# Queue orders pinned from a walk over the traced program, and the sums of a step by seven in two half tiles

## The chip, the cores and the metric

The kernel runs on one core of one Trainium2 chip. The metric is the device time of one execution in microseconds (us), lower is better. The engines are called TensorE (PE in the profile, its weight loader PEld), VectorE (DVE), ScalarE (ACT), GpSimd (POOL) and SyncE (SP, which issues the DMAs of the weights).

## The reference

The reference is a trunk of two decoder layers over one sequence of 256 tokens with 2048 channels, all in float32. Cut to what matters:

```python
def reference(x, ...):
    h = x
    for i in range(2):
        hn = rmsnorm(h, norm_mix[i])
        if i == 0:      # causal means over 2/4/8/16 tokens in 4 channel groups, minus hn, times pool_w
            mix = pool_mixer(hn, pool_w[0], pool_scale[0])
        else:           # 8 heads of differential attention with distance penalties
            mix = diff_attention(hn, w_qkv[0], ..., subln_g[0], w_o[0], lambda_init)
        h = h + mix
        h = h + swiglu(rmsnorm(h, norm_ffn[i]), w_gate[i], w_up[i], w_down[i])
    return rmsnorm(h, final_norm)

def swiglu(h, wg, wu, wd):      # 2048 -> 2 x 5632 -> 2048
    return (jax.nn.silu(h @ wg) * (h @ wu)) @ wd
```

Nearly all of the work is in matrix products with large weights: gate, up and down of two layers (5632 wide), the queries, keys and values (2048 to 6144) and the output projection (2048 to 2048).

## The kernel before, in words

**Numbers in halves.** A float32 operand is split into a high half, rounded to the type fp32r (`whi`, made by ScalarE's copy), and a low half, the difference (`wlo`, made by VectorE). A product a·b becomes three products on TensorE: high·high, high·low and low·high, added up in one PSUM bank (`products`, L172 to L190; the matmul is L189, and each takes 128 rows by 512 columns).

**Steps.** `group` (L147) multiplies two blocks of 128 tokens by two blocks of 512 output columns. It goes through the contracted dimension in steps of 256, that is two blocks of 128. A weight step is one tile `raw` of 128 x 4 x 512 float32 (1 MiB) that holds its four blocks B12, B11, B22, B21; `load` (L116) fetches it by a DMA on SP's queue, into a pool with three buffers. A plain step takes the eight block products in the ordinary way, 8 x 3 = 24 matmuls, into four banks C11, C12, C21, C22. A step by seven (`seven`) forms seven products of sums of blocks (the scheme of Strassen and Winograd), 7 x 3 = 21 matmuls, into seven banks M1, M2, M6, M7, P5, P3, P4. The sums of the weight blocks T1 to T4 are made in float32 by `sums` (L128 to L134, VectorE, one instruction over two blocks, L130, and two over one, L132 and L133) in a tile `tsum` of 128 x 4 x 512, and split by `sum_halves` (L136) into `thi` (L139, ScalarE) and `tlo` (L140, VectorE), one instruction of 2048 columns each. `halves` (L121) splits the raw blocks (L124 ScalarE, L125 VectorE): 2048 columns in a plain step, 1536 in a step by seven, which does not need B12 alone. `combined` (L204) puts the seven or eight banks together on VectorE and ScalarE; of the banks M2, P3, P4 and X the plain steps are C11, C12, C21, C22.

**Buffers.** `raw`, `whi` and `wlo` have three buffers. `tsum` has one. `thi` and `tlo` have one in the feed-forward layers and two in the groups of attention (`bufs=2` in L599, L618 and L637). PSUM has eight banks; M1, M6, M7 and P5 are also the banks that `aux` (L83) hands out in turn for transposes and small products.

**Which steps are by seven.** In the feed-forward layers the steps 2, 4 and 6 of the eight (2 and 4 of six); in the first group of queries and keys, in the first of values and in the output projection 4 and 6; in the other three groups of queries and keys and the second of values the order of the steps is 0, 1, 3, 5, 4, 2, 6, 7 (`LATE`, L46), and 4, 2 and 6 are by seven, one after the other. There are 114 steps by seven in all.

**Stages.** The pooling mixer comes first (L288 to L436, up to some 60 us). A feed-forward layer (`ffn`, L466) goes in three chunks of 4, 4 and 3 groups of 512 hidden columns: for each group the products with gate and up (L483), silu and the product of both (L486, L487), and transposes of the result into operands `h` (`pair`, L254, transposes L259; a pair by seven also gets its own sums, L273 to L275, a high half L276 and a low half L277); after the groups of a chunk come the two halves of the down projection (L502). Attention (L527 to L643) has four groups of queries and keys with two heads each (`head`, L566, transposes L607, scores L576, transposes of the probabilities L561), two groups of values (L618, with L622 to L624 for the heads), and the output projection (L637). `finish` (L440) ends the last down projection for each of the two token blocks t: it adds the products to the residual in `x_tok` (L449), sums squares on ScalarE (L452), multiplies by the final gain into `ys` (L453; an earlier part of it in L516), works out the factor (L229 to L234), scales (L458, L461, L463) and issues the output DMAs (L459, L462, L464).

**What sets the order.** All engines run their queues in order. The kernel traces its instructions in program order; when the context closes, the framework's scheduler orders each engine's queue by priority, which is the program order, shifted by `tc.high_priority` (L429 and L432), and by when its own timing model takes an instruction as ready. So products of a later bank or step can stand ahead of earlier ones on TensorE. It then sets the semaphores. Within one PSUM bank the products stay in program order.

```python
for x, y in ((ah, hi), (ah, lo), (al, hi)):
    left[b] -= 1
    nc.tensor.matmul(ps[b], x, y[:, block], start=first, stop=(left[b] == 0))
    first = False
```

Of the kernel before, what the change touches and what calls it, by code (L numbers as in the profile page):

```python
# [2 lines left out]

# [6 lines left out]
F32 = mybir.dt.float32  # L10
F32R = mybir.dt.float32r
# [5 lines left out]
P = 128  # L17
# [8 lines left out]
EPS = 1e-6  # L26
WARM = 8
LATER = 70

WINDOWS = (2, 4, 8, 16)  # L30

# [19 lines left out]

A22, A21, A11, A12, S1, S3, S2, S4 = range(8)
T1, T3, T2, T4 = range(4)


@with_exitstack
def trunk_kernel(ctx, tc, x_n, gains, scale_in, final_in, subln, lam_in, band, counts_in, dist,
# [39 lines left out]
    def x_at(t, first, count=512):  # L97

        j, off = divmod(first, 512)
        return x_tok[:, j, t, off:off + count]  # L100
# [25 lines left out]
        return hi, lo  # L126

    def sums(pool, raw):  # L128
        t = pool.tile([P, 4, 512], F32, name="tsum")
        nc.vector.tensor_tensor(t[:, T1:T3 + 1], raw[:, B11:B22 + 1],  # L130
                                raw[:, B12:B12 + 1].broadcast_to([P, 2, 512]), ALU.add)
        nc.vector.tensor_tensor(t[:, T2], t[:, T1], raw[:, B22], ALU.add)  # L132
        nc.vector.tensor_tensor(t[:, T4], t[:, T2], raw[:, B21], ALU.add)  # L133
        return t  # L134

    def sum_halves(pool, t, bufs):  # L136
        hi = pool.tile([P, 4, 512], F32R, name="thi", bufs=bufs)
        lo = pool.tile([P, 4, 512], F32R, name="tlo", bufs=bufs)
        nc.scalar.copy(hi, t)  # L139
        nc.vector.tensor_tensor(lo, t, f32(hi), ALU.subtract)  # L140
        return hi, lo
# [298 lines left out]
    def finish(cs, ys, final_sb, ss):  # L440

        for t in range(2):
            part = tmp.tile([P, 64], F32, name="part", bufs=2)
            nc.vector.tensor_reduce(part[:, 0:1], ss[:, t, 0:2], AX.X, ALU.add)
            for b in range(2):
                for h in range(2):
                    first = 1024 + b * 512 + h * S
                    mine = slice(h * S, (h + 1) * S)
                    nc.vector.tensor_tensor(x_at(t, first, S), cs[t][b][:, mine], x_at(t, first, S), ALU.add)  # L449
# [3 lines left out]
                nc.vector.tensor_tensor(ys[1][:, t, b], x_at(t, 1024 + b * 512), final_sb[1][:, b * 512:(b + 1) * 512], ALU.mult)  # L453
# [4 lines left out]
            nc.scalar.activation(ys[1][:, t, 0], ys[1][:, t, 0], AF.Copy, scale=rt)  # L458
            nc.scalar.dma_start(out=out[rows, 1024:1536], in_=ys[1][:, t, 0])  # L459
            for b in range(2):  # L460
                nc.vector.tensor_scalar(ys[0][:, t, b], ys[0][:, t, b], rt, None, ALU.mult)  # L461
            nc.sync.dma_start(out=out[rows, 0:1024], in_=ys[0][:, t].rearrange("p b n -> p (b n)"))  # L462
            nc.vector.tensor_scalar(ys[1][:, t, 1], ys[1][:, t, 1], rt, None, ALU.mult)  # L463
            nc.sync.dma_start(out=out[rows, 1536:2048], in_=ys[1][:, t, 1])  # L464

    def ffn(layer, xq, ss, next_op, next_gain):  # L466

# [2 lines left out]
        with tc.tile_pool(name=f"ffn{layer}", bufs=1, reuse_waits="tile") as hp:  # L470
            g0 = 0
            ys = []
            for c, n in enumerate(CHUNKS):
# [19 lines left out]
                for o in range(2):  # L493
# [13 lines left out]
                    for b, t in ((0, 0), (0, 1), (1, 0), (1, 1)):  # L507
                        j = 2 * o + b
                        nc.vector.tensor_tensor(x_at(t, j * 512), cs[t][b], x_at(t, j * 512), ALU.add)
                        if last:  # L510
                            square_sum(ss_next, t, j)
                        if last and next_op is None:
                            if b == 0 and t == 0:
                                ys.append([hp.tile([P, 2, 2, 512], F32, name="y", tag=("tsum", "thi")[i]) for i in range(2)])
                                ys = ys[0]
                            nc.vector.tensor_tensor(ys[o][:, t, b], x_at(t, j * 512),  # L516
                                                    final_sb[o][:, b * 512:(b + 1) * 512], ALU.mult)
                        if last and t and next_op is not None:
                            transposed(next_op, j, next_gain, SEVEN_QKV)
# [8 lines left out]
    with tc.tile_pool(name="attn", bufs=1, reuse_waits="tile") as ap_, ExitStack() as heads:  # L528
# [67 lines left out]
        for g in range(4):  # L596

            order, by_seven = LATE if g else EARLY
            cs = combined(group([(xp[p], p in by_seven, w_qk[g, p]) for p in order], hq, bufs=2), hq)  # L599
            cs = scaled(cs, (qs_col, r_col))  # L600
            for u in range(2):
                qk = at.tile([P, 2, 2, S], F32, name="qk")
                for b in range(2):
                    tp = aux((P, 2, S))
                    for c in range(2):
                        for t in range(2):
                            nc.tensor.transpose(tp[:, c, t * P:(t + 1) * P],  # L607
                                                cs[t][b][:, (2 * u + c) * P:(2 * u + c + 1) * P], ident)
                    nc.scalar.copy(qk[:, b], tp)
                head(2 * g + u, qk)  # L610
# [4 lines left out]
        oT = [None] * NP  # L615
        for g in range(2):
            order, by_seven = LATE if g else EARLY
            cs = scaled(combined(group([(xp[p], p in by_seven, w_v[g, p]) for p in order], op_, bufs=2), op_), (r_col, r_col))  # L618
            for h in range(4 * g, 4 * g + 4):
                v = [cs[t][h % 4 // 2][:, h % 2 * E:(h % 2 + 1) * E] for t in range(2)]  # L620
                op = aux((P, 2, E))
# [12 lines left out]
                pair(oT[h], lambda i, t: on[:, t, i * P:(i + 1) * P], [gs[:, i:i + 1] for i in range(2)], h in SEVEN_O)  # L634
        xq = operand(SEVEN)
        for g in range(2):
            cs = combined(group([(oT[p], p in SEVEN_O, w_o[g, p]) for p in range(NP)], op_, bufs=2), op_)  # L637
            for b in range(2):
                j = 2 * g + b
                for t in range(2):  # L640
# [2 lines left out]
                transposed(xq, j, 4, SEVEN)  # L643

    ffn(1, xq, ss_next, None, None)


def _steps(w, left, right):
# [85 lines left out]
```

## Time and profile before

| what | value |
|---|---|
| median of 3 runs | 1837.09 us (1836.84 to 1837.28) |
| the profiled execution | 1837.09 us |
| its span, first to last instruction | 1835.3 us |
| TensorE busy in the span | 1823.0 us (99%), 8192 matmuls |
| VectorE busy | 1630.5 us (89%), 1692 instructions |
| ScalarE busy | 1048.7 us (57%), 1026 instructions |
| DMA engines | 193 GB/s of HBM traffic over the span |

TensorE's granted clock was 0.998 of full speed over the span. A row of the waits reads: who waited, for whom, us in total, times, longest. A row of the timeline reads: start, us, engine, line, operation, output and input with shapes, how many were merged, and in brackets the idle time before it and what ended it. TensorE's matmuls overlap in the profile (a 512-column one is shown with 0.39 us), so their pace is read from start to start. A row of groups ends with the busy time and the mean in ns, and with the idle time before the group.

### The profile page before, as it was taken

The page shows a single profiled execution, that of the slowest core. Times are in us where ns is not written, and L with a number is a line of the kernel's source. Part 1 is how long each engine was busy: PE and PEld are TensorE (multiplying, and loading weights), DVE is VectorE, ACT ScalarE, POOL GpSimd, SP SyncE. Part 2 cuts the span into 40 slices and gives each one's busy share as a digit, 9 for nine tenths or more (in the row PEclk, how much of TensorE's full clock was granted, in tenths as well). Part 3 has the DMA queues.
Part 4 walks back from the last instruction along what each step waited for, and adds up shares of the span by engine and source line. Part 5 has one row for each costly group of instructions (what it writes and reads, how often), then busy time and mean ns, then how long its engine had stood idle before and what let it go on. Part 6 is the DMA issues. An engine that isn't in the chain of part 4 may idle for free.

```text
span 1835.3 us, 20926 instructions
## 1 busy us (share of the span) xinstructions
PE 1823.0 (99%) x8192; PEld 1492.3 (81%) x8192; DVE 1630.5 (89%) x1692; ACT 1048.7 (57%) x1026; POOL 0.7 (0%) x6
## 2 busy tenths in 40 slices
PE   9999999999999999999999999999999999999997
PEld 6888888888888888888888888888888888888886
DVE  7999999889899899989988789889899899988986
ACT  6655544555554556666667665555554555555563
POOL 0000000000000000000000000000000000000000
PEclk9999999999999999999999999999999999999999
DMA  7555555555555555544554555555555545556552
GB/s 271 200 184 193 208 196 209 204 187 205 205 194 197 205 184 184 206 173 174 182 183 163 181 184 184 206 185 205 204 190 202 207 183 193 212 215 210 202 189 110
DMA packets 50930, 356.35 MB, mean 194 GB/s; under 512 B 6160, under 2 KB 6288, under 8 KB 8464
## 3 DMA queue, kind: packets, MB, share of 16 engines
q1 hardware_dynamic: 49968, 353.40, 53.5%
q10 hardware_dynamic: 864, 1.63, 0.2%
q8 instruction: 64, 1.05, 0.2%
q14 instruction: 34, 0.28, 0.0%
HBM read 352.90 MB, written 2.10 MB: 193 GB/s over the span
## 4 chain that ended last, share of the span: by engine, by line
PE 97%; DVE 1%; ACT 1%; DMA 0%; issue 0%; SPq 0%; DVEq 0%; ACTq 0%
PE b L189 93%; PE b L259 2%; PE b L576 1%; PE b L607 0%; DMA x_tok<-x_n 0%; PE b L368 0%; PE b L624 0%; PE b L622 0%; PE b L623 0%; PE b L561 0%; DVE wlo L354 0%; DVE xt_hl L252 0%; ACT sq L240 0%; DVE wlo L125 0%; DVE z L392 0%
## 5 line engine op out<-in xcount | busy, mean ns | idle before, releaser
L189 PE MATMUL b<-whi,xp 128*128 128x512 f32 x2784 | 899.4, 392 | 0.0
L124 ACT CAST whi<-raw 128x1536 fp32r<-128x1536 f32 (+1 forms) x328 | 578.7, 1764 | 549.6 <-PE b L189 450.4
L125 DVE TENSOR_TENSOR wlo<-raw,whi 128x1536 fp32r<-128x1536 f32 (+1 forms) x328 | 689.6, 2103 | 159.2 <-ACT whi L124 158.9
L189 PEld LDWEIGHTS b<-whi,xp 128*128 128x128 f32 x2784 | 520.1, 188 | 108.2 <-ACT e L272 0.4
L189 PE MATMUL b<-wlo,xp 128*128 128x512 f32 x1392 | 544.2, 391 | 0.0
L189 PE MATMUL b<-whi,h 128*128 128x512 f32 x1108 | 354.2, 390 | 0.0
L189 PEld LDWEIGHTS b<-wlo,xp 128*128 128x128 f32 x1392 | 261.5, 188 | 53.0
L140 DVE TENSOR_TENSOR tlo<-tsum,thi 128x2048 fp32r<-128x2048 f32 x114 | 260.6, 2286 | 8.3 <-ACT thi L139 8.3
L189 PEld LDWEIGHTS b<-whi,h 128*128 128x128 f32 x1108 | 207.5, 188 | 43.2
L139 ACT CAST thi<-tsum 128x2048 fp32r<-128x2048 f32 x114 | 217.6, 1908 | 19.7 <-DVE tsum L133 17.2
L189 PE MATMUL b<-thi,xp 128*128 128x512 f32 x640 | 223.4, 389 | 0.0
L189 PE MATMUL b<-wlo,h 128*128 128x512 f32 x554 | 215.8, 389 | 0.0
L130 DVE TENSOR_TENSOR tsum<-raw 128x1024 f32<-128x1024 f32 x114 | 139.1, 1220 | 2.1 <-DMA raw<-w_v 0.6
L189 PEld LDWEIGHTS b<-thi,xp 128*128 128x128 f32 x640 | 120.1, 188 | 24.7
L189 PE MATMUL b<-tlo,xp 128*128 128x512 f32 x320 | 125.9, 393 | 0.0
L189 PEld LDWEIGHTS b<-wlo,h 128*128 128x128 f32 x554 | 104.0, 188 | 21.3
L189 PE MATMUL b<-thi,h 128*128 128x512 f32 x240 | 83.7, 390 | 0.0
L133 DVE TENSOR_TENSOR tsum<-tsum,raw 128x512 f32<-128x512 f32 x114 | 78.5, 689 | 2.2
L132 DVE TENSOR_TENSOR tsum<-tsum,raw 128x512 f32<-128x512 f32 x114 | 78.1, 685 | 0.6
L189 PEld LDWEIGHTS b<-tlo,xp 128*128 128x128 f32 x320 | 60.0, 188 | 16.5 <-DVE tlo L140 4.4
L189 PE MATMUL b<-whi,oT 128*128 128x512 f32 x216 | 69.7, 395 | 0.0
L189 PEld LDWEIGHTS b<-thi,h 128*128 128x128 f32 x240 | 45.0, 188 | 9.5 <-ACT thi L139 0.4
(147 smaller groups left out, 1211.7 us busy)
## 6 DMA issues: line engine op xcount, KB each, us to landing
raw<-w_gu SPq DMA_DIRECT2D x176, 1024.0 KB, 4.8
raw<-w_down SPq DMA_DIRECT2D x88, 1024.0 KB, 4.8
raw<-w_qk SPq DMA_DIRECT2D x32, 1024.0 KB, 4.8
raw<-w_v SPq DMA_DIRECT2D x16, 1024.0 KB, 4.8
raw<-w_o SPq DMA_DIRECT2D x16, 1024.0 KB, 4.8
x_tok<-x_n SPq DMA_DIRECT2D x4, 512.0 KB, 6.9
w<-pool_w SPq DMA_DIRECT2D x4, 512.0 KB, 7.5
raw<-pool_w SPq DMA_DIRECT2D x2, 1024.0 KB, 11.1
```

What stands on the lines that cost most here:

```text
L124: nc.scalar.copy(hi[:, lo_block:], raw[:, lo_block:])
L125: nc.vector.tensor_tensor(lo[:, lo_block:], raw[:, lo_block:], f32(hi[:, lo_block:]), ALU.subtract)
L130: nc.vector.tensor_tensor(t[:, T1:T3 + 1], raw[:, B11:B22 + 1], raw[:, B12:B12 + 1].broadcast_to([P, 2, 512]), ALU.add)
L132: nc.vector.tensor_tensor(t[:, T2], t[:, T1], raw[:, B22], ALU.add)
L133: nc.vector.tensor_tensor(t[:, T4], t[:, T2], raw[:, B21], ALU.add)
L139: nc.scalar.copy(hi, t)
L140: nc.vector.tensor_tensor(lo, t, f32(hi), ALU.subtract)
L189: nc.tensor.matmul(ps[b], x, y[:, block], start=first, stop=(left[b] == 0))
L259: nc.tensor.transpose(ps[:, i, 1 - t if seven else t], src(i, t), ident)
L576: nc.tensor.matmul(sc[:, :nk], qk[:, 0, c, qb * P:(qb + 1) * P], qk[:, 1, c, :nk], start=True, stop=True)
```

## The change

The change has three parts.

1. **Orders.** At the end of the trace `in_order_of_need` takes the program's instructions as steps with the steps that each must wait for (`steps_of`: overlapping tiles, whole PSUM banks, buffers that come round again), gives each a duration (`Step`: how long it holds its engine and when its result is there, by engine, operation and size), and runs them in a list schedule (`walk`): the engine that is free first takes, of its steps that are ready, the one of the lowest rank. In the first round the rank is the program order. `due` then works out, backwards from TensorE's order, when each step's result is needed, and the walk is repeated (`ROUNDS = 2`) with that as the rank of VectorE, ScalarE and GpSimd, while TensorE and SP keep the program order. The order with the shortest end is pinned for PE, DVE, ACT and SP by a dependency from each instruction to the one before it on its queue.
2. **Halves of the sums.** `tsum`, `thi` and `tlo` become two tiles of two blocks each (T1 and T3, T2 and T4), each with its own instruction for the high and the low half and its own release. The pools of attention keep one buffer of each where they had two. The order of the seven products changes: M1, M2, P3, then the four on sums; and the four on sums first where the next step is by seven too.
3. **The final tiles** `ys` become one tile for each token block.

```diff
+PE, DVE, ACT, SP, POOL = (...)
+SIGNAL = {PE: 54, DVE: 36, ACT: 36, SP: 36, POOL: 36}
+AGAIN = 70
+SETTLES = {DVE: 36, ACT: 120}
+LANDING = 2100
+PER_MIB = 2500
+
+class Step:
+    def __init__(self, k, ins=None):
...
+        n = max(size(a) for a in list(ins.outs) + list(ins.ins) if hasattr(a, "ap"))
+        if self.dma:
+            self.share = PER_MIB * bytes_ / 2 ** 20
+            self.holds, self.lasts = (60 if self.engine == ACT else 330), LANDING + self.share
+        elif self.engine == PE:
+            n = size(ins.outs[0])
+            one = 110 if ins.is_transpose else 14 + n / 2.4 if "float32r" in str(ins.ins[0].dtype) else 14 + n / 0.6
+            self.holds, self.lasts = one, one + 163
+        elif self.engine == DVE:
...
+                self.lasts = 152 + n / (1.92 if ins.opcode == "TensorCopy" else 0.96)
+            self.holds = max(self.lasts - 80, 60)
+        elif self.engine == ACT:
+            self.lasts = 165 + n * 0.852
...
+def walk(steps, rank):
...
+    for _ in steps:
+        now, e = min((free[e] if able[e] else max(free[e], coming[e][0][0]), i)
+                     for i, e in enumerate(engines) if able[e] or coming[e])
+        e = engines[e]
+        while coming[e] and coming[e][0][0] <= now:
+            k = heapq.heappop(coming[e])[1]
+            heapq.heappush(able[e], (rank[k], k))
+        s = steps[heapq.heappop(able[e])[1]]
...
+        if len(waits) > 1 and ready[s.k] > free[e]:
+            now += AGAIN
+        start[s.k], free[e] = now, now + s.holds
...
+def due(steps, start):
+    by_start = sorted(steps, key=lambda s: start[s.k])
+    at, clock = {}, 0.0
+    for s in by_start:
+        if s.engine == PE:
+            at[s.k], clock = clock, clock + s.holds
+    limit = [0.0] * len(steps)
+    for s in reversed(by_start):
+        limit[s.k] = min([limit[k] - s.lasts - SIGNAL[steps[k].engine] for k in s.after] + [at.get(s.k, clock)])
+    return limit
+
+def in_order_of_need(tc):
+    steps = steps_of(list(tc.nc.cur_bb.bb.instructions))
+    rank = [float(s.k) for s in steps]
+    start, end = walk(steps, rank)
+    for _ in range(ROUNDS):
+        limit = due(steps, start)
+        rank = [float(s.k) if s.engine in (PE, SP) else limit[s.k] for s in steps]
+        again, span = walk(steps, rank)
+        if span < end:
+            start, end = again, span
+    order = mybir.DependencyInfo(mybir.DependencyClass.NoSync, mybir.DependencyReason.DATA)
+    for e in (PE, DVE, ACT, SP):
+        line = sorted((s for s in steps if s.engine == e), key=lambda s: start[s.k])
+        for one, two in zip(line, line[1:]):
+            tc.add_manual_dep(two.ins, one.ins.name, order, reason="order of need")
+    return start, end, steps
...
     def sums(pool, raw):
-        t = pool.tile([P, 4, 512], F32, name="tsum")
-        nc.vector.tensor_tensor(t[:, T1:T3 + 1], raw[:, B11:B22 + 1],
-                                raw[:, B12:B12 + 1].broadcast_to([P, 2, 512]), ALU.add)
-        nc.vector.tensor_tensor(t[:, T2], t[:, T1], raw[:, B22], ALU.add)
-        nc.vector.tensor_tensor(t[:, T4], t[:, T2], raw[:, B21], ALU.add)
-        return t
-
-    def sum_halves(pool, t, bufs):
-        hi = pool.tile([P, 4, 512], F32R, name="thi", bufs=bufs)
-        lo = pool.tile([P, 4, 512], F32R, name="tlo", bufs=bufs)
+        s, t = (pool.tile([P, 2, 512], F32, name=f"tsum{i}") for i in range(2))
+        nc.vector.tensor_tensor(s, raw[:, B11:B22 + 1], raw[:, B12:B12 + 1].broadcast_to([P, 2, 512]), ALU.add)
+        nc.vector.tensor_tensor(t[:, 0], s[:, 0], raw[:, B22], ALU.add)
+        nc.vector.tensor_tensor(t[:, 1], t[:, 0], raw[:, B21], ALU.add)
+        return s, t
+
+    def sum_halves(pool, t, bufs, i):
+        hi = pool.tile([P, 2, 512], F32R, name=f"thi{i}", bufs=bufs)
+        lo = pool.tile([P, 2, 512], F32R, name=f"tlo{i}", bufs=bufs)
...
-        for a, seven, src in steps:
-            if seven:
-                plan.append([(M1, [(A11, 0, B11)]), (M2, [(A12, 0, B21)]), (M6, [(S2, 1, T2)]), (M7, [(S3, 1, T3)]),
-                             (P5, [(S1, 1, T1)]), (P3, [(S4, 0, B22)]), (P4, [(A22, 1, T4)])])
+        for n, (a, seven, src) in enumerate(steps):
+            if seven and n + 1 < len(steps) and steps[n + 1][1]:
+                plan.append([(P5, [(S1, 1, 0)]), (M7, [(S3, 1, 1)]), (M6, [(S2, 2, 0)]), (P4, [(A22, 2, 1)]),
+                             (M1, [(A11, 0, B11)]), (M2, [(A12, 0, B21)]), (P3, [(S4, 0, B22)])])
+            elif seven:
+                plan.append([(M1, [(A11, 0, B11)]), (M2, [(A12, 0, B21)]), (P3, [(S4, 0, B22)]), (P5, [(S1, 1, 0)]),
+                             (M7, [(S3, 1, 1)]), (M6, [(S2, 2, 0)]), (P4, [(A22, 2, 1)])])
...
-                w.append(sum_halves(pool, t, bufs))
+                w += [sum_halves(pool, t[i], bufs, i) for i in range(2)]
...
-                                ys.append([hp.tile([P, 2, 2, 512], F32, name="y", tag=("tsum", "thi")[i]) for i in range(2)])
-                                ys = ys[0]
+                                ys.extend([hp.tile([P, 2, 512], F32, name="y", tag=f"{n}{i}") for i in range(2)]
+                                          for n in ("tsum", "thi"))
...
-            cs = combined(group([(xp[p], p in by_seven, w_qk[g, p]) for p in order], hq, bufs=2), hq)
+            cs = combined(group([(xp[p], p in by_seven, w_qk[g, p]) for p in order], hq, bufs=1), hq)
...
+    in_order_of_need(tc)
```

More of the change, by code (lines that the diff above doesn't have):

```diff
@@ L1 @@
+import heapq
 import math
@@ L28 @@
 LATER = 70
+ROUNDS = 2
 WINDOWS = (2, 4, 8, 16)
@@ new lines, in steps_of @@
+def steps_of(instructions):
+    steps, seen, slots, users, gates = [], {}, {}, {}, {}
+    open_, closed, pool_of = [], None, {}
+    for ins in instructions:
+        if ins.opcode == "TilePoolBoundary":
+            if ins.op == "release":
+                past = Step(len(steps))
+                past.before = {k for n in seen if pool_of.get(n) == open_[-1] for k in users[n]}
+                past.before |= {closed} if closed is not None else set()
+                closed = past.k
+                steps.append(past)
+                open_.pop()
+                continue
+            open_.append(len(pool_of))
+            pool_of.update((t.name, open_[-1]) for t in ins.bass_pool_tiles or ())
+            continue
+        if not any(hasattr(a, "bass_ap") for a in ins.outs):
+            continue
+        step = Step(len(steps), ins)
+        for writes, args in ((False, ins.ins), (True, ins.outs)):
+            for a in args:
+                ap = getattr(a, "bass_ap", None)
+                if ap is None or not hasattr(ap.tensor, "tag"):
+                    continue
+                t, dims = ap.tensor, [tuple(d) for d in ap.ap]
+                first = ap.offset % dims[0][0]
+                last = first + sum((c - 1) * s for s, c in dims[1:])
+                alone = writes
+                if t.space == PSUM:
+                    first, last, alone = 0, 511, True
+                if t.name not in seen:
+                    seen[t.name], users[t.name], gate = [], [], set()
+                    line = slots.setdefault(t.tag, [])
+                    bufs = t.bufs or t.tag_meta.bufs
+                    if len(line) >= bufs:
+                        gate.update(users[line[-bufs]])
+                    elif t.name in pool_of and closed is not None:
+                        gate.add(closed)
+                    if line:
+                        gate.add(users[line[-1]][0])
+                    line.append(t.name)
+                    gates[t.name] = gate
+                own = {k for f, l, w, k, _ in seen[t.name] if (w or alone) and f <= last and first <= l}
+                step.before |= own or gates[t.name]
+                step.reads.update(k for f, l, _, k, w in seen[t.name] if w and not writes and f <= last and first <= l)
+                if alone:
+                    seen[t.name] = [s for s in seen[t.name] if s[0] < first or s[1] > last or s[3] == step.k]
+                seen[t.name].append((first, last, alone, step.k, writes))
+                users[t.name].append(step.k)
+        step.before.discard(step.k)
+        steps.append(step)
+    for s in steps:
+        for k in s.before:
+            steps[k].after.append(s.k)
+    return steps
@@ new lines, in walk @@
+def walk(steps, rank):
+    missing = [len(s.before) for s in steps]
+    ready, start = [0.0] * len(steps), [0.0] * len(steps)
+    engines = (PE, DVE, ACT, SP, POOL)
+    free, wire = {e: 0.0 for e in engines}, 0.0
+    known, count = {e: {} for e in engines}, {e: 0 for e in engines}
+    place = [0] * len(steps)
+    able, coming = {e: [] for e in engines}, {e: [] for e in engines}
+    for s in steps:
+        if not s.before:
+            heapq.heappush(coming[s.engine], (0.0, s.k))
+    for _ in steps:
[6 more added lines that the diff above has]
+        s = steps[heapq.heappop(able[e])[1]]
+        waits = {}
+        for k in s.before:
+            t = steps[k].engine
+            if place[k] > max(waits.get(t, 0), known[e].get(t, 0)) and (t != e or e != PE):
+                waits[t] = place[k]
+        known[e].update(waits)
+        count[e] += 1
+        place[s.k] = count[e]
+        if len(waits) > 1 and ready[s.k] > free[e]:
+            now += AGAIN
+        start[s.k], free[e] = now, now + s.holds
+        end = now + s.lasts
+        if s.dma:
+            begin = max(now + s.holds, wire)
+            wire = begin + s.share
+            end = begin + s.lasts
+        for k in s.after:
+            t = steps[k].engine
+            if t != e or s.dma:
+                at = end + SIGNAL[t]
+            elif e == DVE or e == ACT and s.k in steps[k].reads:
+                at = end + SETTLES[e]
+            else:
+                at = now + s.holds
+            ready[k] = max(ready[k], at)
+            missing[k] -= 1
+            if not missing[k]:
+                heapq.heappush(coming[steps[k].engine], (ready[k], k))
+    return start, max(free.values())
@@ L617, in trunk_kernel @@
             order, by_seven = LATE if g else EARLY
-            cs = scaled(combined(group([(xp[p], p in by_seven, w_v[g, p]) for p in order], op_, bufs=2), op_), (r_col, r_col))
+            cs = scaled(combined(group([(xp[p], p in by_seven, w_v[g, p]) for p in order], op_, bufs=1), op_), (r_col, r_col))
             for h in range(4 * g, 4 * g + 4):
```

38 lines of the change are left out of this document (29 added, 9 removed).

## The prediction, made before the result was known

> **What bounds the kernel now.** I read the page's engine totals, its chain of work that ended last, the waits of TensorE and of its weight loader, and then the timeline at the places that those name.
>
> ```profile
> span 1835.3 us, 20926 instructions
> PE 1823.0 (99%) x8192; PEld 1492.3 (81%) x8192; DVE 1630.5 (89%) x1692; ACT 1048.7 (57%) x1026; POOL 0.7 (0%) x6
> ...
> PE 97%; DVE 1%; ACT 1%; DMA 0%; issue 0%; SPq 0%; DVEq 0%; ACTq 0%
> ```
>
> The span is TensorE's. The profiled execution took 1837.09 us, which is also the median of the three runs (1836.84 to 1837.28), and 1.8 us more than its span; so the sum below is made on 1837.09. VectorE's 89% stands close behind. A stretch of the chain without a foreign wait gives TensorE's pace:
>
> ```profile
> 220.75 124.33 PE b L189 x547
> ```
>
> 124.33 us / 547 = 0.2273 us from one 512-column product to the next. No product is added or removed by the change, so it can only win what lies between products, before the first or behind the last. The weight loader's waits, asked for three parts of the span, say how much that is. They are the loader's, which runs a little ahead of the products, and so are an upper bound for the array itself. The first row is from 100 to 700 us, the next five from 700 to 1175 (attention), the last from 1175 to 1835:
>
> ```profile
> PEld b L189 <- DVE tlo L140: 3.3, 8, 0.4
> ...
> PEld b L607 <- ACT c L551: 2.2, 7, 0.4
> PEld b L561 <- DVE a_sb L592: 2.2, 8, 0.4
> PEld b L259 <- ACT o_n L632: 2.1, 8, 0.4
> PEld b L576 <- ACT qk L609: 1.5, 8, 0.2
> PEld b L576 <- ACT aT L563: 1.0, 3, 0.4
> ...
> PEld b L189 <- DVE tlo L140: 3.3, 8, 0.4
> ```
>
> In the two feed-forward layers there is one wait alone: sixteen times for tlo, the low half of a step by seven. In attention there are some 9 us of loader's waits, of 0.2 to 0.4 us each. Everything else is the pace itself. So the prize is a few us of 1837, and 0.2% (3.7 us), about what a measurement of this kernel can tell from no change, is the line that matters.
>
> **The wait for tlo.** One of the sixteen, on the timeline (TensorE and VectorE):
>
> ```profile
> 1560.28 1.22 DVE L277 TENSOR_TENSOR h<-e,h 128x1024 fp32r<-128x1024 f32 x1
> 1561.42 2.28 DVE L140 TENSOR_TENSOR tlo<-tsum,thi 128x2048 fp32r<-128x2048 f32 x1
> ...
> 1562.69 0.84 PE L189 MATMUL b<-thi,h 128*128 128x512 f32 x3
> 1563.37 0.39 PE L189 MATMUL b<-whi,h 128*128 128x512 f32 x1
> 1563.62 1.75 DVE L125 TENSOR_TENSOR wlo<-raw,whi 128x1536 fp32r<-128x1536 f32 x1
> 1563.76 0.50 PE L189 MATMUL b<-tlo,h 128*128 128x512 f32 x1
> 1564.09 0.39 PE L189 MATMUL b<-thi,h 128*128 128x512 f32 x1
> 1564.32 0.40 PE L189 MATMUL b<-tlo,h 128*128 128x512 f32 x1
> 1564.55 0.40 PE L189 MATMUL b<-thi,h 128*128 128x512 f32 x1
> 1564.79 0.39 PE L189 MATMUL b<-tlo,h 128*128 128x512 f32 x1
> ```
>
> At the first step by seven of a group VectorE is late: h's own low half comes first, then tlo, then wlo. TensorE has spent all the products that need only high halves and stands. From 1563.37 to 1563.76 is 0.39 us instead of 0.227, then 0.33: 0.16 + 0.11 = 0.27 us lost. The change acts on this in three ways: tlo comes in two instructions of 1024 columns, so the first is done about 1.1 us sooner; the products on sums move behind M1, M2 and P3; and VectorE's queue is sorted by due time, which can put h's low half (needed tens of us later) behind tlo. The slack is larger than the 0.27 us by each of them alone. **Term: 16 x 0.27 = -4.3 us.** Bounds: 0 if the pinned order puts the same instruction last, -6.6 if the loader's whole 2 x 3.3 us were the array's. I take -4.3, worked out from the array's own rows.
>
> **What the halves cost.** Prices by form:
>
> ```profile
> L140 DVE TENSOR_TENSOR tlo<-tsum,thi 128x2048 fp32r<-128x2048 f32 x114 | 260.6, 2286 | 8.3 <-ACT thi L139 8.3
> L125 DVE TENSOR_TENSOR wlo<-raw,whi 128x1536 fp32r<-128x1536 f32 x114 | 199.8, 1753 | 3.4 <-ACT whi L124 3.1
> L130 DVE TENSOR_TENSOR tsum<-raw 128x1024 f32<-128x1024 f32 x114 | 139.1, 1220 | 2.1 <-DMA raw<-w_v 0.6
> L133 DVE TENSOR_TENSOR tsum<-tsum,raw 128x512 f32<-128x512 f32 x114 | 78.5, 689 | 2.2
> ...
> L139 ACT CAST thi<-tsum 128x2048 fp32r<-128x2048 f32 x114 | 217.6, 1908 | 19.7 <-DVE tsum L133 17.2 <-PE b L189 2.5
> L276 ACT CAST h<-e 128x1024 fp32r<-128x1024 f32 x16 | 16.7, 1044 | 0.0
> ```
>
> The sums stay three instructions. VectorE: 2 x 1.220 - 2.286 = 0.154 us more for each of 114 steps, 17.6 us; ScalarE: 2 x 1.044 - 1.908 = 0.18, 20.5 us. Both lie beside TensorE's work: VectorE goes from 89% to 90%, ScalarE from 57% to 58%. **Term: 0.** The cover is gone only where VectorE has no slack (the slower rival). The true price on VectorE is lower than the durations say: tlo starts at 1561.42 while the instruction before it, 1560.28 + 1.22, ends at 1561.50. The Trainium skill speaks against the split: "VectorE: DVE Perf Modes", section "The DRAIN you can't avoid", has the next instruction wait until the pipe is empty, with an earlier start only where nothing holds it, so by the strict reading the whole 17.6 us is added to the queue; the trace's overlap of 0.08 us leaves 0.07 of the 0.154, 8 us. Neither is on the path by the sum above.
>
> Two more tiles a step also mean two more first uses, each with a semaphore that TensorE must see: 228 of them. No row prices a wait that is already met; the last products above stand 0.23 and 0.24 us apart, so 0 to 0.01 us each. **Term: 228 x 0.005 = +1.1 us**, the middle, with bounds 0 and +2.3. What is queued behind such a wait is TensorE's whole queue; a half that comes late is priced as the tlo wait above.
>
> **The start and the transposes.** TensorE's stops before 40 us, and a place where transposes are taken one by one:
>
> ```profile
> 22.00 0.40 PE L368 MATMUL b<-whi,xt_hl 128*128 128x512 f32 x1
> 23.08 0.50 PE L368 MATMUL b<-whi,xt_hl 128*128 128x512 f32 x1 [0.69 <-DVE y_hl L252]
> ...
> 31.96 0.40 PE L368 MATMUL b<-wlo,xt_hl 128*128 128x512 f32 x1
> 32.98 0.73 PE L368 MATMUL b<-whi,xt_hl 128*128 128x512 f32 x2 [0.62 <-DVE xt_hl L252]
> ...
> 57.41 0.27 PE L259 MATMUL b<-ident,x_tok 128*128 128x128 f32 x1
> 57.43 0.48 PE L189 MATMUL b<-whi,xp 128*128 128x512 f32 x1
> 57.75 0.27 PE L259 MATMUL b<-ident,x_tok 128*128 128x128 f32 x1
> ...
> 1553.60 0.82 PE L259 MATMUL b<-ident,c 128*128 128x128 f32 x6
> ```
>
> The two stops cost 1.08 - 0.23 and 1.02 - 0.23, 1.6 us together. They come from VectorE's order (a low half of y or of pool weights ahead of the operand that TensorE wants next), which due times address. **Term: -1.2 us**; bounds -1.6 and +1.6, since a new order can miss as often. The product behind a transpose starts 0.32 us before what follows it (57.43 to 57.75) instead of 0.227: 0.09 us for each return from transposes to products. Between 57 and 64 us there are a dozen such single transposes. The walk lets four transposes into one bank follow each other without a pause, so I take half of the returns away: **-0.5 us**. In a feed-forward group there are two bursts (2 transposes, then the 6 at 1553.60), because half t = 0 is ready earlier; by the walk's rule, earliest in the program first among the ready, that stays so: 0, with the bound that each burst splits once more, 22 groups x 2 x 0.09 = +4.0 us.
>
> **Attention, queues, tail.** The attention waits of 0.2 to 0.4 us follow chains between three engines. The walk's order will remove some and create others: 0, bounds half of the 9 us either way. SP's loads stay in program order and still wait for raw, POOL is not pinned; 0. At the end, the last product on the timeline and two pieces of the chain:
>
> ```profile
> 1825.38 0.39 PE L189 MATMUL b<-whi,h 128*128 128x512 f32 x1
> ```
> ```profile
> 1825.35 0.69 DVE y L453
> 1826.05 0.34 DVE x_tok L449
> ```
>
> The last add could start when the last product is done, 1825.77, and starts behind y at about 1825.96: at most 0.2 us to win; the chain from there to the landing of the output is unchanged. **-0.1 us.**
>
> **Sum:** -4.3 + 1.1 - 1.2 - 0.5 - 0.1 = -5.0 us, 1837.1 - 5.0 = **1832.1 us**.
>
> **Rivals.** *No change that shows.* The tlo waits go, but the order by program position takes transposes as soon as each is ready. One more return in each of 22 feed-forward groups and two more for each of 8 heads is 38 x 0.09 = 3.4 us; -5.0 + 3.4 = -1.6, **1835.5 us**. For it: the walk charges nothing for a return. Against: the present order already has the two bursts per group. Chance 0.26. *The change does not do what it says*: the pinned order comes out as today's, or misses tlo by as much, and only the extra first uses and the tail remain: 1837.1 + 1.0 = **1838.1 us**, chance 0.06.
>
> *Slower: VectorE becomes the bound where three steps by seven follow each other* (order 4, 2, 6 in three groups of queries and keys and one of values). VectorE needs 1.753 + 1.220 + 2 x 0.689 + 2 x 1.220 = 6.8 us for such a step, TensorE 21 x 0.2273 = 4.8 us, so the run lives on what was made ahead. Before, two sets of thi and tlo stood in these pools; now one, in two halves, so one step's halves (2 x 1.22 = 2.44 us) move from ahead of the run into it. Unhidden that is 4 x 2.44 = 9.8 us; -5.0 + 9.8 = +4.8, **1841.9 us**. It decides from the point where VectorE has no idle left in a group; the stretch from 838 to 886 us has this:
>
> ```profile
> 838.00:886.00 48.00, 48.00 (x224) 38.18 (x223) 43.83 (x68) 30.33 (x43) 0.00 (x0) 1.00 0.52 177
> ```
>
> 4.2 us are idle in 48 (the third pair is VectorE's), more than 2.44, and the new order uses the sums first, so the halves come free 9 products (2.0 us) before the step ends. That speaks against it. By the rule of the Trainium skill's "VectorE: DVE Perf Modes" above the run would hold 3 x 0.15 us more on VectorE, too little to change this. Chance 0.15.
>
> **How the numbers follow.** The forecast has the remaining 0.53, with its own range from 1827.5 (start and half of attention's bound won too) to 1834.5. Faster by over 0.2% is below 1833.4 us: nearly the whole forecast, 0.51. Within 0.2%: the upper end of the forecast and the two middle cases, 0.34. Slower: 0.15. The range of 8 in 10 goes from 1827.5, leaving out some 0.06 below, to 1840.0, leaving out most of the slower rival.
>
> **What would show it.** Right: tlo gone from the weight loader's waits in both feed-forward stretches; VectorE at x1806 and ScalarE at x1140 (114 more each), TensorE still x8192; no idle in brackets at TensorE's rows around 23 and 33 us; the bursts of transposes not more than two per feed-forward group. Wrong, towards no change: as many products at 0.32 us as a third burst per group makes. Wrong, towards slower: longer stretches of the attention groups, with TensorE waiting for tlo or thi inside the run 4, 2, 6. Wrong altogether: new idle of TensorE in the feed-forward layers for wlo or whi, which would mean that the walk's times don't hold there.

## The result, and the profile after

The changed kernel takes 1826.88 us (median of 4 runs, 1826.55 to 1827.15) against 1836.96 us of the kernel before (4 runs, 1836.77 to 1837.28): 10.1 us less, ratio 0.9945 with a 95% interval of 0.9928 to 0.9962. The prediction was 1832.1 us with a range from 1827.5 to 1840.0: right in sign, with half of the size, and the result lies 0.6 us below the range.

The page of the changed kernel, its totals and its chain (L379 is now the line of the products, L449 of the transposes into operands):

```profile
span 1825.1 us, 21208 instructions
...
PE 1813.2 (99%) x8192; PEld 1496.3 (82%) x8192; DVE 1629.1 (89%) x1806; ACT 1055.6 (58%) x1140; POOL 0.7 (0%) x6
...
PE 99%; DMA 0%; ACT 0%; DVE 0%; issue 0%; DVEq 0%; SPq 0%; ACTq 0%
```

The counts are as forecast: 114 more instructions on VectorE and on ScalarE, 8192 on TensorE. VectorE's busy time did not grow. The split itself shows in its groups by form:

```profile
L327 DVE TENSOR_TENSOR tlo<-tsum,thi 128x1024 fp32r<-128x1024 f32 x228 | 273.9, 1217 | 1.1 <-ACT thi L326 0.8
...
L326 ACT CAST thi<-tsum 128x1024 fp32r<-128x1024 f32 x228 | 235.6, 1049 | 147.1 <-DVE tsum L320 116.4 <-DVE tsum L318 26.0 <-PE b L379 3.7
```

273.9 - 260.6 = 13 us more of durations on VectorE and 235.6 - 217.6 = 18 us on ScalarE, off the path. Up to 34.51 us the chain of the kernel before went through DMA, ScalarE and VectorE; its longest piece, and the last ones before TensorE takes over, in part:

```profile
2.58 7.68 DMA x_tok<-x_n
...
28.98 0.74 DVE z L392
29.73 2.20 DVE wlo L125
...
32.52 0.79 DVE xt_hl L252 x2
...
34.51 1.06 PE b L259 x8
```

Now, behind one weight DMA, it is TensorE alone from 6.56 us on, as far as the window to 70 us shows:

```profile
1.18 5.24 DMA w<-pool_w
6.42 0.14 issue
6.56 1.95 PE b L554 x4
8.51 0.87 PE b L529 x8
9.39 5.15 PE b L554 x12
...
18.85 5.59 PE b L558 x24
```

The weight loader's waits between 100 and 700 us and between 1170 and 1825 us are empty lists now: no tlo, nothing else. In attention (700 to 1170 us) seven rows with 3.2 us are left, where ten rows held 11.0 us before. The four longest:

```profile
PEld b L449 <- ACT o_n L822: 1.1, 1, 1.1
PEld b L766 <- ACT qk L799: 0.5, 3, 0.2
PEld b L379 <- DVE c L407: 0.4, 2, 0.2
PEld b L797 <- DVE s_sb L768: 0.4, 2, 0.2
```

The waits for `c` of the heads (L607 before), for a_sb and for aT, 5.4 us in three rows before, are not among the seven. The longest one left also stops TensorE itself:

```profile
981.55 0.33 PE L449 MATMUL b<-ident,o_n 128*128 128x128 f32 x1 [0.73 <-ACT o_n L822]
```

To see where the time went, I cut each trace at the start of TensorE's first instruction, of the 366th, the 3024th and the 4500th product of the line L189 (L379 in the changed kernel), of the last product, and at the end of the span. The 3024th is the last product of the first feed-forward layer and the 4500th the last of attention. The first cut lies inside the first feed-forward layer: the stage called start holds the pooling mixer and the first 365 products of that layer, about two of its eleven groups of gate and up, and all sixteen waits for tlo that the prediction counts lie behind it. TensorE's own work in each stage is its count of instructions by their paces from start to start in the trace: 0.227 us a product, 0.109 a transpose, 0.108, 0.216 and 0.429 for float32 products of 128, 256 and 512 columns, and 0.213 for each of the 16 small ones that open the kernel. The pace of a product is rounded: the spacings below 0.23 us have a mean of 0.2267 us, by which the own work is 0.1, 0.9, 0.5 and 1.0 us less in the four stages. So a distance from it is known to about a us, and differences between two kernels are better known.

| kernel | us | start | feed-forward 1 | attention | feed-forward 2 | tail |
|---|---|---|---|---|---|---|
| TensorE's own work | | 123.5 | 613.8 | 372.4 | 699.2 | |
| before | 1836.96 | 128.4 | 616.6 | 377.7 | 701.7 | 9.9 |
| changed | 1826.88 | 125.4 | 614.1 | 375.5 | 699.2 | 9.8 |
| no_pins | 1832.52 | 128.7 | 613.8 | 377.3 | 699.8 | 9.9 |
| pins_only | 1829.26 | 125.7 | 614.2 | 377.2 | 699.7 | 9.7 |
| no_due | 1827.29 | 125.7 | 614.2 | 375.6 | 699.2 | 9.8 |
| old_products | 1829.89 | 125.4 | 614.1 | 378.0 | 699.7 | 9.8 |
| whole_new | 1829.42 | 125.5 | 613.8 | 378.2 | 699.0 | 9.7 |
| new_products | 1845.39 | 129.0 | 620.3 | 379.3 | 704.0 | 9.9 |
| halves_nopins | 1844.40 | 129.5 | 614.0 | 388.8 | 699.3 | 10.0 |
| halves_two | 1833.88 | 129.4 | 614.0 | 378.1 | 699.4 | 9.9 |
| pin_pe | 1856.29 | 137.4 | 614.6 | 392.4 | 700.1 | 9.9 |
| pin_rest | 1842.01 | 134.9 | 614.1 | 379.8 | 699.4 | 9.8 |
| scattered | 1829.21 | 126.1 | 614.9 | 375.7 | 699.9 | 9.8 |
| bursts | 1827.82 | 125.7 | 614.3 | 376.6 | 699.0 | 9.8 |
| two_bufs | 1826.17 | 125.4 | 613.7 | 375.4 | 699.0 | 9.7 |

The change wins 3.0 us at the start, 2.4 and 2.5 us in the feed-forward layers, 2.2 us in attention, 0.1 us in the tail. The feed-forward layers (614.1 and 699.2 us) stand at TensorE's own work as far as its pace is known. Of the 3.0 us at the start, 2.4 are won before 36 us. The other rows are the experiments; each was timed beside the kernel before, whose medians lay between 1836.96 and 1837.10 us.

### The profile page after: what moved, and what is told of

It is laid out like the page before. It is cut to its first block, busy times and chain, and to the rows that moved or that the text cites. A ratio compares the mean times of both kernels' runs of the same rounds, so it can differ in the third digit from the quotient of the medians.

```text
span 1825.1 us, 21208 instructions
## 1 busy us (share of the span) xinstructions
PE 1813.2 (99%) x8192; PEld 1496.3 (82%) x8192; DVE 1629.1 (89%) x1806; ACT 1055.6 (58%) x1140; POOL 0.7 (0%) x6
## 4 chain that ended last, share of the span: by engine, by line
PE 99%; DMA 0%; ACT 0%; DVE 0%; issue 0%; DVEq 0%; SPq 0%; ACTq 0%
PE b L379 94%; PE b L449 2%; PE b L558 1%; PE b L554 1%; PE b L766 1%; PE b L797 0%; DMA w<-pool_w 0%; PE b L812 0%; PE b L813 0%; PE b L814 0%; PE b L751 0%; PE b L529 0%; PE b L571 0%; PE b L575 0%; PE b L573 0%; ACT L420 0%
## 5 line engine op out<-in xcount | busy, mean ns | idle before, releaser
L379 PE MATMUL b<-whi,xp 128*128 128x512 f32 x2784 | 884.1, 392 | 0.0
L379 PEld LDWEIGHTS b<-whi,xp 128*128 128x128 f32 x2784 | 520.6, 188 | 107.5 <-DVE c L407 0.4
L379 PE MATMUL b<-wlo,xp 128*128 128x512 f32 x1392 | 545.2, 392 | 0.0
L379 PE MATMUL b<-whi,h 128*128 128x512 f32 x1108 | 348.4, 390 | 0.0
L326 ACT CAST thi<-tsum 128x1024 fp32r<-128x1024 f32 x228 | 235.6, 1049 | 147.1 <-DVE tsum L320 116.4
L379 PEld LDWEIGHTS b<-wlo,xp 128*128 128x128 f32 x1392 | 261.5, 188 | 52.6
L327 DVE TENSOR_TENSOR tlo<-tsum,thi 128x1024 fp32r<-128x1024 f32 x228 | 273.9, 1217 | 1.1 <-ACT thi L326 0.8
L379 PEld LDWEIGHTS b<-whi,h 128*128 128x128 f32 x1108 | 207.6, 188 | 43.0
L379 PE MATMUL b<-wlo,h 128*128 128x512 f32 x554 | 216.3, 390 | 0.0
L379 PE MATMUL b<-thi,xp 128*128 128x512 f32 x640 | 211.0, 389 | 0.0
L379 PEld LDWEIGHTS b<-thi,xp 128*128 128x128 f32 x640 | 120.1, 188 | 24.9
L379 PE MATMUL b<-tlo,xp 128*128 128x512 f32 x320 | 124.6, 389 | 0.0
L379 PEld LDWEIGHTS b<-wlo,h 128*128 128x128 f32 x554 | 104.0, 188 | 21.1
L379 PE MATMUL b<-thi,h 128*128 128x512 f32 x240 | 78.9, 389 | 0.0
L676 ACT ACTIVATE c<-c,r_tok 128x512 f32<-128x512 f32 x44 | 31.9, 725 | 71.9 <-DVE c L402 61.5
L379 PEld LDWEIGHTS b<-tlo,xp 128*128 128x128 f32 x320 | 60.1, 188 | 12.5
L379 PE MATMUL b<-whi,oT 128*128 128x512 f32 x216 | 69.0, 395 | 0.0
```

The lines of the kernel that those rows point to most:

```text
L676: nc.scalar.activation(gate, gate, AF.Silu, scale=r[:, t:t + 1])
```

## The experiments

**Which part does it.** Four kernels were run first. The first two take the change apart.

no_pins:

```diff
-    in_order_of_need(tc)
```

> The changed kernel without the pinned orders: the half tiles, the new order of the seven products and the single buffers stay, the framework's scheduler sets the queues. Theory 1 (the orders do it: the stops come from orders worked out with other latencies than the chip's): stops come back in the feed-forward layers, 1833 to 1838 us. Theory 2 (halves and product order do it, the pins only help start and attention): both feed-forward layers keep their 5 us, start and attention lose theirs, about 1832 us.

1832.52 us, ratio 0.9976 (0.9966 to 0.9985). The feed-forward layers keep their gain, start and attention lose theirs, as theory 2 has it. Its first stops are those of the kernel before (y_hl, xt_hl, xt_hl), on its timeline of 17 to 36 us:

```profile
23.33 0.50 PE L558 MATMUL b<-whi,xt_hl 128*128 128x512 f32 x1 [0.82 <-DVE y_hl L442]
33.22 0.74 PE L558 MATMUL b<-whi,xt_hl 128*128 128x512 f32 x2 [0.63 <-DVE xt_hl L442]
34.76 1.06 PE L449 MATMUL b<-ident,x_tok 128*128 128x128 f32 x8 [0.33 <-DVE xt_hl L442]
```

The third of them in the kernel before, which the prediction did not price:

```profile
34.51 1.06 PE L259 MATMUL b<-ident,x_tok 128*128 128x128 f32 x8 [0.34 <-DVE xt_hl L252]
```

pins_only: the file before with `Step`, `steps_of`, `walk`, `due`, `in_order_of_need` and

```diff
     ffn(1, xq, ss_next, None, None)
+    in_order_of_need(tc)
```

> The kernel before with the pinned orders alone: whole tiles of the sums, the old order of the seven products, two buffers in attention. Theory 1 (orders): 1827 to 1829 us, no wait for tlo. Theory 2 (halves and product order): the wait for tlo at the first step by seven stays, 4 to 5 us above the changed kernel, 1831 to 1832 us.

1829.26 us, ratio 0.9957 (0.9945 to 0.9970): the feed-forward layers are nearly at TensorE's work with whole tiles too (one wait for tlo of 0.4 us is left to the weight loader), and the start is won. Theory 1 holds for the pins, 0.3 us above its range, theory 2 for the halves and the product order. Either ends nearly all of the wait for tlo, so their gains, 7.8 and 4.6 us, do not add: together it is 10.1.

no_due:

```diff
-ROUNDS = 2
+ROUNDS = 0
```

> The changed kernel with the first walk alone: VectorE and ScalarE take, among what is ready, the earliest in the program instead of the earliest due. TensorE's order comes out the same. If the due times carry the gain, as the prediction argued for tlo and the start: 1829 to 1833 us, with waits for low halves at the first step by seven of each group. If TensorE's order and the walk's latencies carry it: 1826.5 to 1828 us.

1827.29 us, ratio 0.9946 (0.9933 to 0.9960), 0.4 us above the changed kernel's median, which was measured at another time. TensorE's order is the same on both traces, instruction for instruction. With the halves and the new product order in place the due times bring little; no run has the pins without them and with whole tiles.

**Halves, product order and pins one by one.** Four more kernels complete the eight combinations; attention has one buffer of thi and tlo in those with halves, as in the change, and two in those with whole tiles.

new_products (no pins, whole tiles):

```diff
-                plan.append([(M1, [(A11, 0, B11)]), (M2, [(A12, 0, B21)]), (M6, [(S2, 1, T2)]), (M7, [(S3, 1, T3)]),
-                             (P5, [(S1, 1, T1)]), (P3, [(S4, 0, B22)]), (P4, [(A22, 1, T4)])])
+                plan.append([(M1, [(A11, 0, B11)]), (M2, [(A12, 0, B21)]), (P3, [(S4, 0, B22)]), (P5, [(S1, 1, T1)]),
+                             (M7, [(S3, 1, T3)]), (M6, [(S2, 1, T2)]), (P4, [(A22, 1, T4)])])
```

> The kernel before with nothing but M1, M2, P3 ahead of the four products on sums; no pins, whole tiles. The prediction held that each of its three ways suffices alone to end the wait for tlo: then both feed-forward layers lose 2.1 to 2.7 us each, about 1832.5 us. If the order alone is not enough, TensorE stops at the same place for the same instruction: 1836 to 1837.5 us.

1845.39 us, ratio 1.0048 (1.0035 to 1.0060): 8.4 us slower, which neither expectation held. Its weight loader waits between 100 and 700 us:

```profile
PEld b L189 <- DVE tlo L140: 5.8, 18, 0.4
PEld b L189 <- DVE c L217: 3.4, 8, 0.9
```

Eighteen waits for tlo instead of eight, and a new one for `c` of L217, the instruction that frees the bank P3. M6 comes sixth in this order instead of third, and what `combined` does to P3 stands behind what it does to M6; that link is read from the code, no run isolates it.

halves_nopins (old product order): `sums`, `sum_halves` and the final tiles as in the change, one buffer, no call of `in_order_of_need`, and

```diff
-                plan.append([(M1, [(A11, 0, B11)]), (M2, [(A12, 0, B21)]), (M6, [(S2, 1, T2)]), (M7, [(S3, 1, T3)]),
-                             (P5, [(S1, 1, T1)]), (P3, [(S4, 0, B22)]), (P4, [(A22, 1, T4)])])
+                plan.append([(M1, [(A11, 0, B11)]), (M2, [(A12, 0, B21)]), (M6, [(S2, 2, 0)]), (M7, [(S3, 1, 1)]),
+                             (P5, [(S1, 1, 0)]), (P3, [(S4, 0, B22)]), (P4, [(A22, 2, 1)])])
```

> The kernel before with the half tiles alone (one buffer, old order of the products, no pins). If halves alone end the wait for tlo: about 1832.5 us. If not, the wait is for the first half instead of the whole, half as long or as long as before: 1835 to 1837 us.

1844.40 us, ratio 1.0041 (1.0028 to 1.0053): 7.4 us slower, outside both. The feed-forward layers do reach TensorE's work, so halves alone end that wait; but attention takes 11.1 us more than before. TensorE's own waits, first row, and the first of the four on the timeline:

```profile
PE b L376 <- DVE tlo L327: 7.0, 4, 1.8
```
```profile
836.37 0.50 PE L376 MATMUL b<-tlo,xp 128*128 128x512 f32 x1 [1.73 <-DVE tlo L327]
```

The other three stand at 886.06, 935.73 and 1037.28 us. By the count of products before them there is one wait near the end of each of the four groups with three steps by seven in a row. Cut by the same count, the second to fourth group of queries and keys take 49.4, 49.7 and 50.4 us instead of 47.0, 47.6 and 47.4. The four waits are 7.0 of the 11.1 us; the rest is spread over shorter stops.

halves_two tests the cause, the single buffer:

```diff
-            cs = combined(group([(xp[p], p in by_seven, w_qk[g, p]) for p in order], hq, bufs=1), hq)
+            cs = combined(group([(xp[p], p in by_seven, w_qk[g, p]) for p in order], hq, bufs=2), hq)
```

and the same in the groups of values and of the output projection.

> Half tiles alone, no pins, old order of the products, but two buffers in attention. The same with one buffer lost 11 us in attention (388.8 us against 377.7 us). Theory: it is the prediction's slower rival, the single buffer in the run of three steps by seven; then attention is back at about 377 us and the whole at 1832 to 1833 us. Rival: the framework's order came out badly for another reason; then attention stays near 388 us, 1842 to 1845 us.

1833.88 us, ratio 0.9983 (0.9974 to 0.9992); attention is back at 378.1 us and the row for tlo is gone. So this is the prediction's slower rival, at 10.6 us for its 9.8. In no_pins, with the new order of the products and one buffer, attention stands at 377.3 us: the order hides it. No run tells its two parts apart, sums first within a run and M1, M2, P3 first elsewhere.

old_products (pins, halves): the change with the plan of halves_nopins.

> The changed kernel with pins and half tiles, but the seven products in the old order (M1, M2, M6, M7, P5, P3, P4). Attention gained 2.2 us with both parts and 0.4 us with either alone. Theory H (the halves give it, with the pins): attention stays at 375.5 us, 1827 us in all. Theory O (the order of the products gives it, sums first where the next step is by seven too): attention back to 377.2 us, about 1829 us.

1829.89 us, ratio 0.9962 (0.9950 to 0.9975).

whole_new (pins, whole tiles, two buffers): pins_only with

```diff
+            if seven and n + 1 < len(steps) and steps[n + 1][1]:
+                plan.append([(P5, [(S1, 1, T1)]), (M7, [(S3, 1, T3)]), (M6, [(S2, 1, T2)]), (P4, [(A22, 1, T4)]),
+                             (M1, [(A11, 0, B11)]), (M2, [(A12, 0, B21)]), (P3, [(S4, 0, B22)])])
```

and the order of new_products otherwise.

> The kernel before with pins and the new order of the products, but whole tiles of the sums and two buffers in attention. Theory H: 1829 us, as with the pins alone. Theory O: about 1827 us, attention 375.5 us.

1829.42 us, ratio 0.9960 (0.9946 to 0.9973). Attention is 378.0 us in old_products and 378.2 in whole_new: each theory fails in one of them, and of these eight kernels only the one with pins, halves and order together wins the 2.2 us there. old_products was not run with two buffers; its trace has 0.9 us of the weight loader's waits for tlo in attention and 2.3 for whi, so the single buffer may be a part of its loss. Each partial kernel keeps a few stops at other places, for instance a half of weights in old_products and a low half in whole_new (two timelines):

```profile
834.69 0.74 PE L376 MATMUL b<-whi,xp 128*128 128x512 f32 x2 [0.72 <-ACT whi L312]
```
```profile
923.69 0.50 PE L380 MATMUL b<-tlo,xp 128*128 128x512 f32 x1 [0.90 <-DVE tlo L328]
```

**Pinning some queues only.** pin_pe:

```diff
-    for e in (PE, DVE, ACT, SP):
+    for e in (PE,):
```

> The changed kernel with TensorE's order alone pinned; the framework orders the other engines around it. If TensorE's own order carries what the pins bring (2.7 us at the start, 2 us in attention): 1827 to 1828.5 us. If the orders of VectorE and ScalarE carry it: 1830 to 1833 us.

1856.29 us, ratio 1.0106 (1.0092 to 1.0120), far outside both expectations. pin_rest:

```diff
-    for e in (PE, DVE, ACT, SP):
+    for e in (DVE, ACT, SP):
```

> The changed kernel with the orders of VectorE, ScalarE and SP pinned and TensorE's left to the framework. TensorE's order alone made everything slower (1856 us), so the pins work as a set or through the other engines. If the others' orders carry the 2.7 us at the start and the 2 us in attention: 1826.5 to 1828.5 us, and TensorE's order hardly matters. If the orders only fit together: TensorE waits for operands that the others make in another order, as with TensorE's pinned alone, over 1832 us.

1842.01 us, ratio 1.0025 (1.0015 to 1.0036), as the second expectation has it. The waits of TensorE, the first rows of pin_pe, then of pin_rest:

```profile
PE b L571 <- ACT xp L466: 5.3, 1, 5.3
PE b L751 <- DVE a_sb L782: 4.3, 3, 3.4
PE b L449 <- ACT o_n L822: 3.1, 2, 2.4
```
```profile
PE b L379 <- DVE wlo L313: 6.5, 4, 2.4
```

The start takes 137.4 us with TensorE pinned, 134.9 with the others pinned, 128.7 with none and 125.4 with all. Split in these two ways the orders lose; all four together win. The rows fit this reading: an order on one queue is right for the times at which the other queues deliver, and the framework's orders deliver at other times.

**The price of a return from transposes.** A return is a step from a transpose to a product. scattered changes the choice in `walk` so that TensorE takes no second transpose while a product is ready (394 returns instead of 118 by the plan); bursts lets the first transpose into a bank wait for the operands of all of that bank (66). The traces have 405 and 69 steps from a transpose to a 512-column product, the changed kernel's 121 and that of the kernel before 119. Of the two edits, in part:

```diff
+        if e == PE and alone and steps[pick[1]].ins.is_transpose:
+            others = [x for x in able[e] if not steps[x[1]].ins.is_transpose]
...
+                pick = min(others)
...
+            alone = s.ins.is_transpose
```
```diff
+            bursts.setdefault(s.ins.outs[0].bass_ap.tensor.name, []).append(s)
+    for burst in bursts.values():
+        own = {s.k for s in burst}
+        for s in burst[1:]:
+            burst[0].before |= s.before - own
```

> The changed kernel with a walk in which TensorE never takes two transposes in a row when a product is ready: 394 returns from a transpose to a product instead of 118. By the prediction's price of 0.09 us a return: 276 x 0.09 = 25 us more, about 1852 us. By the other reading (the product behind a transpose is only shown early, by as much as its row is longer, and the return is free): 1826 to 1828 us.

> The changed kernel with a walk in which the first transpose into a bank waits until all of that bank can go: 66 returns from transposes to products instead of 118. By the prediction's 0.09 us a return: 52 x 0.09 = 4.7 us less, 1822 us. By the price that the scattered transposes bound, 2.3 us / 276 = 0.008 us: 0.4 us less, and what later transposes cost comes on top: 1826 to 1828 us.

scattered 1829.21 us, ratio 0.9956 (0.9943 to 0.9970): 1.2 us above the expectation of free returns, and 2.3 us above the changed kernel for 276 more returns, not 25. bursts 1827.82 us, ratio 0.9951 (0.9938 to 0.9963): not a us less for 52 fewer returns but 0.9 more, and attention is 1.1 us longer (376.6 us): later transposes can lengthen its chains, which no run isolates. A return costs at most 2.3 / 276 = 0.008 us, if nothing else got shorter in scattered. On its timeline:

```profile
1546.41 0.27 PE L460 MATMUL b<-ident,c 128*128 128x128 f32 x1
1546.43 0.48 PE L390 MATMUL b<-whi,h 128*128 128x512 f32 x1
1546.75 0.27 PE L460 MATMUL b<-ident,c 128*128 128x128 f32 x1
```

From transpose to transpose it is 0.34 us, and a transpose and a product are 0.109 + 0.227 = 0.336 us. The product's 0.32 us to what follows is paid back by the 0.03 us between the transpose and the product.

**The better version.** two_bufs is the change with `bufs=2` in the three groups of attention.

> The changed kernel with two buffers of thi and tlo in attention instead of one. If the single buffer costs anything under the pins, attention gets shorter than 375.5 us: 1825 to 1826.5 us. If the pinned order hides it: within 0.5 us of 1826.9 us.

1826.17 us, ratio 0.9941 (0.9929 to 0.9954), 5 runs from 1826.05 to 1826.18: 0.7 us below the changed kernel's median, which was measured at another time, and outside its four runs' span. The time is in the range of the first expectation, but not for its reason: attention gives 0.1 us of it and the feed-forward layers, whose buffers are as they were, 0.6 us, so its cause is open.

## Why the prediction was wrong

The bound, the counts, the tlo term and the tail were right, and all four of its signs of being right appeared. The sum missed 5.2 us: attention by 2.2, start and returns by 1.3, the first uses by up to 1.1, tlo by 0.6. Two steps failed. The gain in attention was put at nothing, though its waits were read. And the start was read from two stops, by "Everything else is the pace itself". The terms that win add up to 6.1 us, while the kernel before stood 15.5 us above TensorE's own work in its four stages.

- **Attention, 0: measured -2.2 us**, the largest single miss. The step "the walk's order will remove some and create others" failed: it removed most, and the longest stop that TensorE has there now is the 0.73 us for o_n. 377.7 - 372.4 = 5.3 us of distance became 3.1. pins_only, with 377.2, behaves as that step said; the gain takes halves and product order too.
- **Start, -1.2 us and returns, -0.5 us: measured -3.0 us together.** Returns were never a cost, and there are as many as before, 121 for 119, so the start's own term was mis-sized by 1.8 us. The stops at 23 and 33 us, which the prediction priced at 1.6 us, went entirely, and so did the third at 34.51 us and smaller ones behind it. The sum over quoted stops was less than the stage's distance from TensorE's own work, 128.4 - 123.5 = 4.9 us.
- **First uses, +1.1 us: between 0 and 0.5 us.** In the feed-forward layers 94 of the 114 steps by seven bring 188 of the first uses. two_bufs (halves) takes 613.7 and 699.0 us there, whole_new (whole tiles) 613.8 and 699.0; the changed kernel takes 0.5 us more than whole_new in the two together. The prediction took the middle of 0 and 0.01 us from spacings of 0.23 and 0.24 us, rounded, beside products that wait; the low end was nearer.
- **tlo, -4.3 us: right.** The feed-forward layers won 4.9 us, and the wait is gone from both. That each of the three ways suffices alone is right for the halves (halves_nopins) and wrong for the order of the products (new_products, 8.4 us slower); the pins end nearly all of it with whole tiles (pins_only), and due times by themselves were not run.
- **The slower rival** was the right mechanism with the right price (9.8 us forecast, 10.6 measured between halves_nopins and halves_two). Of the two reasons against it, 4.2 us of VectorE's idle in a group did not hide it in halves_nopins; the new order of the products does (no_pins), and so do the pins (old_products loses 0.3 us against before where halves_nopins loses 11.1).
- **The rival of no change** stood on returns at 0.09 us and falls with them. The strict reading of the Trainium skill's "VectorE: DVE Perf Modes", section "The DRAIN you can't avoid", would put 17.6 us on VectorE's queue; VectorE's busy time, in which overlapping rows count once, went from 1630.5 to 1629.1 us, so the trace does not show it.
- **The range** ended at 1827.5, 0.6 us above the result. Its lower end is not what its words give: 0.4 us more at the start and half of attention's bound of 4.5 us make 1829.4, all of that bound 1827.2. The first uses at 0 and a gain beyond the two quoted stops of the start were in neither.

Open: most of the 3.1 us in attention (0.7 is the stop for o_n) and of the 1.9 us at the start (0.7 is the wait for the first pool weights, in front of 6.56 us) that remain above TensorE's own work, and why attention needs all three parts.

## What to carry to other kernels

Where one engine is busy nearly throughout, first subtract its own work, count by pace, from each stage: the difference is what an order can win there, and single rows of stops show only part of it. Take the pace to more digits than the rows show, since it is multiplied by thousands. Orders of queues belong together: pinning a part of them against another planner's made this kernel 5 to 19 us slower than the kernel before, and without pins the halves with one buffer cost 7 us, the product order alone 8 us, while both together won 5. Before a row's length is taken as a cost, the rows around it must be added up from start to start.

## What the runs showed of the hardware

A 512-column product right behind a transpose is shown 0.08 us too early: it starts 0.03 us after the transpose and stands 0.32 us before its successor, and the pair takes 0.34 us. Behind a float32 product of 256 columns it starts after 0.03 us and stands 0.42 us before its successor, together 0.447 us against the 0.216 + 0.227 us of both (twelve places on the changed kernel's trace). So TensorE changes between the two kinds at no cost above 0.01 us. Waits for semaphores that are met cost TensorE next to nothing: on the traces two_bufs has 758 of them on weight loads in the feed-forward layers, the changed kernel 795 and whole_new 674, at 1312.7, 1313.3 and 1312.8 us.
